# Column order and a 64-byte shift in the row-wise matrix products of a one-layer hybrid decoder

## Chip, cores and metric

The kernel runs on one core of one Trainium2 chip. The metric is the device time of one execution in microseconds (us), taken as the median of several runs.

## What is computed

One decoder layer on 256 tokens of width 2048, all in float32. The input projection has 5728 columns, the output projection maps 2048 to 2048, and the MLP goes from 2048 to 8192 and back. These four products are nearly all of the arithmetic:

```python
def hybrid_layer(x, g_mix, w_in, ..., w_out, g_mlp, w_up, w_down):
    h = rmsnorm(x, g_mix) @ w_in                 # 2048 x 5728
    ...
    x = x + jnp.concatenate([y_ssd, y_att], axis=-1) @ w_out   # 2048 x 2048
    u = rmsnorm(x, g_mlp) @ w_up                 # 2048 x 8192
    return x + jnp.square(jax.nn.relu(u)) @ w_down   # 8192 x 2048
```

Between the input and the output projection lie a state-space scan with a short convolution, and an attention over the 64 keys that a small indexer picks. The change touches neither.

## The kernel before

**Three matmuls for one.** A float32 product is computed with matmuls on the type `float32r`. Each operand is split into a high part that this type holds exactly and a low part that is the remainder, and each product becomes three: high by high, low by high, high by low. The weights come from memory as float32 in tiles named `raw`; `operands` (L113) loads them with a DMA on SP's queue (L122), ScalarE (ACT) writes the high part (L125) and VectorE (DVE) the low part (L126), both into one tile `w2`. There are 4 buffers of `raw` and 5 of `w2`, so the weights of several steps are ready ahead of TensorE.

**Two kinds of product.** In `product` (L138) the tokens end up on partitions: the stationary operand is 128 columns of activations (`hx`, `yah`, `ysh` or `uh`, with their low parts), the moving operand is the weights, 512 columns of a row of `w2` (304 in the two blocks `m0` and `m1` of the input projection), and the result is one accumulator of 512 columns in PSUM for each half of the tokens. For each of 16 slices `kt` of the inner dimension it issues six matmuls, L148 to L150 for the first 128 tokens and again for the others; one `operands` call serves two slices, that is 12 matmuls. In `product_t` (L184) it is the other way round: 128 columns of weights are stationary, and 256 tokens move (L200).

**Blocks.** The input projection is the blocks `k`, `m0`, `qi` (four calls of `product_t`), `xbc` (six calls), `m1`, `q0`, `q1`, `z0` and `z1`. Then come four blocks of `w_out`, 32 calls of `product_t` for `w_up` and 16 blocks of `product` for `w_down`. So 25 blocks of `product` are 512 columns wide, at 96 matmuls each, and two are 304 columns wide, also at 96. The last block of `w_down` is special: it has a `tail`, is cut into halves of 256 columns, and keeps four slices back so that its rows can leave early.

**Places.** Every large tile that TensorE reads (`hx`, `x2x`, `uh`, `ul`, `yah`, `yal`, `ysh`, `ysl`, `kih`, `kil`, `qis`, and each buffer of `w2`) starts at byte 224 of a 256-byte stretch of its partition; two unused tiles (L217, L219) see to that for the long-lived ones. A `shift` moves the weights inside `w2`: by 16 columns (64 bytes) for `product_t` (L188), by 48 columns for the block with the tail (L158), and by none for all other blocks of `product`. Below, the *place* of a matmul is the start of its moving operand minus the start of the next matmul's stationary operand, within 256 bytes. It is 0 in the 512-wide blocks of `product`, minus 64 in `product_t` and in the halves of the tail block, 0 for the indexer's matmuls (L465, and L466 for the most part), and in the 304-wide blocks, whose rows are not a whole number of 256 bytes, it goes through 0, minus 64, plus 64 and 128.

The order of TensorE's work is written out by hand: `step()` lets side tasks (transposes, the scan, the attention) put their matmuls between those of the products.

Of the kernel before, what the change touches and what calls it, by code (L numbers as in the profile page):

```python
# [9 lines left out]
F32 = mybir.dt.float32  # L10
F32R = mybir.dt.float32r
I32 = mybir.dt.int32
AF = mybir.ActivationFunctionType
OP = mybir.AluOpType
AX = mybir.AxisListType

P = 128
# [12 lines left out]
WB = 5  # L30
RB = 4

SPARE = 64
SHIFT_T = 16


Z0, XBC0, DT0, Q0, K0, V0, QI0, KI0, WI0, END = (
# [31 lines left out]
def hymba_kernel(ctx: ExitStack, tc: tile.TileContext, xn, xt, w_in, w_out, w_up, w_down, vcol, vrow, out):  # L69
    nc = tc.nc  # L70
    ctx.enter_context(tc.manual_schedule(engines={nc.tensor.engine}))
    keep = ctx.enter_context(tc.tile_pool(name="keep", bufs=1))
    wts = ctx.enter_context(tc.tile_pool(name="wts", bufs=1))
# [24 lines left out]
    def step():  # L98
        for t in list(tasks):
            if isinstance(t[1], int) and t[1] > 0:  # L100
                t[1] -= 1
            elif not isinstance(t[1], str) or t[1] in done:
                advance(t)
# [6 lines left out]
        return vc[:, VC[name] + i:VC[name] + i + 1]  # L110


    def operands(src, n, load=None, shift=0):  # L113

        with tc.high_priority(offset=HP):
            raw = wts.tile([P, n], F32, name="raw", tag="raw", bufs=RB)
            both = wts.tile([P, 2 * n + SPARE], F32R, name="w2", tag="w2", bufs=WB)
            hi, lo = both[:, shift:shift + n], both[:, shift + n:shift + 2 * n]
            step = n if load is None else n // 2
            for i in range(0, n, step):  # L120
                s = slice(i, i + step)
                nc.sync.dma_start(raw[:, s], src[:, s])  # L122
                if load is not None:
                    load()
                nc.scalar.copy(hi[:, s], raw[:, s])  # L125
                nc.vector.tensor_tensor(lo[:, s], raw[:, s], hi[:, s].bitcast(F32), op=OP.subtract)  # L126
        return hi, lo

    other = []
# [1 line left out]
    def mp(name):  # L131
        other.append(name)
        return ps.tile([P, 512], F32, name=name, tag="mid")

    def accumulator():
        return ps.tile([P, 512], F32, name="acc", tag="acc")

    def product(src, n, left, load=None, tail=None):  # L138


        acc = [accumulator(), accumulator()]
        last = KT if tail is None else KT - 4

        def part(kt, out, b, wh, wl):
            s = slice(b * P, (b + 1) * P)
            ah, al = left(kt)
            free = tail is not None
            nc.tensor.matmul(out, ah[:, s], wh, start=(kt == 0), stop=False, skip_group_check=free)  # L148
            nc.tensor.matmul(out, al[:, s], wh, start=False, stop=False, skip_group_check=free)  # L149
            nc.tensor.matmul(out, ah[:, s], wl, start=False, stop=(kt == KT - 1), skip_group_check=free)  # L150

        kept = []
        halves = [slice(0, n // 2), slice(n // 2, n)]
        if tail is not None:
            acc.append(mp("acc_t"))
        for kt in range(KT):
            if kt % 2 == 0:
                hi, lo = operands(src[kt // 2], 2 * n, load, 0 if tail is None else SPARE - SHIFT_T)  # L158
            w = slice(kt % 2 * n, kt % 2 * n + n)
            wh, wl = hi[:, w], lo[:, w]  # L160
            if tail is None:
                for b in range(NB):
                    part(kt, acc[b][:, :n], b, wh, wl)
            elif kt < last:
                for c in halves if kt else [slice(0, n)]:
                    part(kt, acc[0][:, c], 0, wh[:, c], wl[:, c])
                for i, c in enumerate(halves):
                    part(kt, acc[1 + i][:, c], 1, wh[:, c], wl[:, c])
            else:
                kept.append((kt, wh, wl))  # L170
            step()
        if tail is not None:
            for kt, wh, wl in kept:
                for c in halves:
                    part(kt, acc[0][:, c], 0, wh[:, c], wl[:, c])
            tail(0, slice(0, n), acc[0])
            for i, c in enumerate(halves):
                for kt, wh, wl in kept:
                    part(kt, acc[1 + i][:, c], 1, wh[:, c], wl[:, c])
                tail(1, c, acc[1 + i][:, c])  # L180
        other.append("product")
        return acc

    def product_t(src, right):  # L184

        acc = accumulator().rearrange("p (c t) -> p c t", c=2)
        for i in range(4):
            hi, lo = operands(src[i], 1024, shift=SHIFT_T)  # L188
            c = i % 2
            for k in range(8):  # L190
                kt = 8 * (i // 2) + k
                x = right(kt)
                s = slice(k * P, (k + 1) * P)
                todo = [(hi, 0, 0, T), (lo, 0, 0, T), (hi, 0, T, T)]

                if other:
                    other.clear()
                    todo[:1] = [(hi, 0, 0, P), (hi, P, P, T - P)]
                for j, (w, at, fr, n) in enumerate(todo):
                    nc.tensor.matmul(acc[:, c, at:at + n], w[:, s], x[:, fr:fr + n], start=(i + k + j == 0),  # L200
                                     stop=(i >= 2 and k == 7 and j == len(todo) - 1), skip_group_check=True)
                if k % 4 == 3:
                    step()
        return acc
# [47 lines left out]
    for name, cols in IN_BLOCKS:  # L252
        n = sum(b - a for a, b in cols)
# [3 lines left out]
    def in_block(name, load=None):  # L257
        o, n = in_off[name]
        src = w_in[o:o + n * D].rearrange("(g p c) -> g p c", g=8, p=P)
        return product(src, n, h_left, load)  # L260

    def in_pair(name, i):
        o = in_off[name][0] + i * 256 * D
        return product_t(w_in[o:o + 256 * D].rearrange("(h p c) -> h p c", h=4, p=P), lambda kt: hx[:, kt, :])
# [430 lines left out]
    def run():  # L695
# [58 lines left out]
        for j in range(4):  # L754
            spawn(residual(j, product(w_out[j], 512, y_left)), f"res{j}")
# [4 lines left out]
    def x2(kt):  # L760
        if kt >= KT - 4:
            need("res3")
        return box[0][:, kt, :]

    first = product_t(w_up[0], x2)
    while tasks:
        step()
# [11 lines left out]
    def up(q):  # L779
        uh = mlp.tile([P, KT, T], F32R, name="uh")  # L780
        ul = mlp.tile([P, KT, T], F32R, name="ul")
        for j in range(8):
            r = mlp.tile([P, 2, T], F32, name="r")
            acc = first if q + j == 0 else product_t(w_up[8 * q + j], x2)
            nc.scalar.activation(r, acc, AF.Relu)
            nc.vector.tensor_tensor(r, r, acc, op=OP.mult)
            s = slice(2 * j, 2 * j + 2)
            nc.scalar.copy(uh[:, s, :], r)
            nc.vector.tensor_tensor(ul[:, s, :], r, uh[:, s, :].bitcast(F32), op=OP.subtract)
        return uh, ul  # L790

    def down(q, u):
        for j in range(4):

            def add(b, c, acc):
                c = slice(512 * j + c.start, 512 * j + c.stop)
                nc.vector.scalar_tensor_tensor(xr[:, b, c], acc, rs4[:, b:b + 1], xr[:, b, c], op0=OP.mult, op1=OP.add)  # L797
                if q == 3:
                    nc.sync.dma_start(out[b * P:(b + 1) * P, c], xr[:, b, c])

            end = q == 3 and j == 3
            acc = product(w_down[4 * q + j], 512, lambda kt: (u[0][:, kt, :], u[1][:, kt, :]), tail=add if end else None)
            for b in range(0 if end else NB):
                add(b, slice(0, 512), acc[b])
# [58 lines left out]
```

## Time and profile before

| What | us |
|---|---|
| Median of 3 runs | 1092.11 (1091.97 to 1092.82) |
| The profiled execution, its own time | 1092.74 |
| Its span, first to last instruction | 1090.7 |
| TensorE busy in the span | 1084.6 (99%) |
| DVE busy | 657.5 (60%) |
| ACT busy | 526.6 (48%) |

TensorE is busy all the time by this table, but the duration of a matmul row holds its way through the array, which overlaps with the next matmul. What one matmul costs a full engine is the distance from its start to the next start, and that is what is read below from the timeline. The trace has lost a few records (7098 matmul rows of the program's 7214), so distances are taken from stretches without a gap.

### The profile page before, as it was taken

What the parts mean: (1) busy time and instruction counts of PE and PEld (TensorE: products, weight loads), DVE (VectorE), ACT (ScalarE), POOL (GpSimd) and SP (SyncE); (2) the same over time, 40 slices, a digit from 0 to 9 for tenths busy, and PEclk for the clock granted to TensorE, in tenths of its full rate; (3) what the DMA queues carried; (4) which work ended last, traced back from release to release, by engine and by line L of the source; (5) the groups of instructions that cost most, each with busy time, mean ns of one, the idle gap of its engine ahead of it and who ended that gap; (6) DMA issues with size and microseconds to landing.
All of it is one profiled execution on the core that took longest, in us unless ns stands there. A gap on an engine that the chain in (4) does not pass through costs nothing.

```text
span 1090.7 us, 17557 instructions
## 1 busy us (share of the span) xinstructions
PE 1084.6 (99%) x7098; PEld 987.5 (91%) x7098; DVE 657.5 (60%) x907; ACT 526.6 (48%) x693; POOL 24.3 (2%) x30
## 2 busy tenths in 40 slices
PE   9999999999999999999999999999999999999998
PEld 7999999888888899999998889998889999888888
DVE  6776898677765565555554455555445555454443
ACT  7745455456755454444443334444334444333331
POOL 0020000122000000000000000000000000000000
PEclk9999999999999999999999999999999999999999
DMA  9865447543475566666666666666666666666662
GB/s 311 272 207 179 153 127 223 165 145 126 135 251 191 176 187 196 195 193 194 195 193 194 193 193 193 193 194 193 194 193 193 193 194 193 194 193 193 213 213 76
DMA packets 63744, 207.52 MB, mean 190 GB/s; under 512 B 7216, under 2 KB 11568, under 8 KB 63664
## 3 DMA queue, kind: packets, MB, share of 16 engines
q1 hardware_dynamic: 63520, 206.36, 59.8%
q8 instruction: 55, 0.90, 0.4%
q14 instruction: 25, 0.20, 0.1%
q10 hardware_dynamic: 144, 0.05, 0.0%
HBM read 204.29 MB, written 2.10 MB: 189 GB/s over the span
## 4 chain that ended last, share of the span: by engine, by line
PE 95%; DVE 2%; DMA 1%; ACT 1%; issue 1%; SPq 0%; ACTq 0%; DVEq 0%
PE acc L200 41%; PE acc L148 16%; PE acc L150 16%; PE acc L149 16%; DVE w L126 1%; PE ps_y L575 1%; DMA xrow<-in_xn 1%; PE ps_sr L659 0%; PE ps_l L613 0%; PE ps_o L638 0%; DMA raw<-in_w_in 0%; ACT xrow L245 0%; DMA xT<-in_xt 0%; PE ps_s L465 0%; PE ps_s L466 0%
## 5 line engine op out<-in xcount | busy, mean ns | idle before, releaser
L126 DVE TENSOR_TENSOR w<-raw,w 128x1024 fp32r<-128x1024 f32 (+3 forms) x400 | 466.4, 1168 | 403.2 <-ACT w L125 402.7
L125 ACT CAST w<-raw 128x1024 fp32r<-128x1024 f32 (+3 forms) x400 | 399.8, 1003 | 504.0 <-PE acc L150 256.3
L200 PE MATMUL acc<-x2x,w 128*128 128x256 f32 (+1 forms) x3077 | 349.8, 276 | 0.0
L200 PEld LDWEIGHTS acc<-x2x,w 128*128 128x128 f32 x3077 | 349.4, 188 | 0.2
L148 PE MATMUL acc<-w,uh 128*128 128x512 f32 (+1 forms) x527 | 199.9, 379 | 0.0
L149 PE MATMUL acc<-w,ul 128*128 128x512 f32 (+1 forms) x527 | 199.8, 379 | 0.0
L150 PE MATMUL acc<-w,uh 128*128 128x512 f32 (+1 forms) x527 | 199.8, 379 | 0.0
L150 PEld LDWEIGHTS acc<-w,uh 128*128 128x128 f32 x527 | 98.9, 188 | 18.8
L149 PEld LDWEIGHTS acc<-w,ul 128*128 128x128 f32 x527 | 98.9, 188 | 18.7
L148 PEld LDWEIGHTS acc<-w,uh 128*128 128x128 f32 x527 | 98.9, 188 | 18.6
L200 PE MATMUL acc<-hx,w 128*128 128x256 f32 (+1 forms) x978 | 115.0, 277 | 0.0
L200 PEld LDWEIGHTS acc<-hx,w 128*128 128x128 f32 x978 | 112.8, 188 | 0.0
L148 PE MATMUL acc<-w,hx 128*128 128x512 f32 (+1 forms) x224 | 85.0, 379 | 0.4 <-ACT w L125 0.4
L150 PE MATMUL acc<-w,hx 128*128 128x512 f32 (+1 forms) x224 | 82.0, 366 | 0.0
L149 PE MATMUL acc<-w,hx 128*128 128x512 f32 (+1 forms) x224 | 81.9, 366 | 0.0
L148 PEld LDWEIGHTS acc<-w,hx 128*128 128x128 f32 x224 | 42.2, 189 | 7.2 <-ACT w L125 0.8
L150 PEld LDWEIGHTS acc<-w,hx 128*128 128x128 f32 x224 | 42.2, 188 | 7.0 <-DVE w L126 0.4
L149 PEld LDWEIGHTS acc<-w,hx 128*128 128x128 f32 x224 | 42.2, 188 | 6.6 <-issue 0.7
L797 DVE SCALAR_TENSOR_TENSOR xr<-acc,rs,xr 128x512 f32<-128x512 f32 (+1 forms) x32 | 22.3, 736 | 9.2 <-PE acc L150 9.2
L148 PE MATMUL acc<-w,yah 128*128 128x512 f32 x64 | 25.7, 402 | 0.0
L148 PE MATMUL acc<-w,ysh 128*128 128x512 f32 x64 | 25.1, 392 | 0.0
L150 PE MATMUL acc<-w,yah 128*128 128x512 f32 x64 | 25.0, 391 | 0.0
(214 smaller groups left out, 663.1 us busy)
## 6 DMA issues: line engine op xcount, KB each, us to landing
raw<-in_w_up SPq DMA_DIRECT2D x128, 512.0 KB, 4.3
raw<-in_w_down SPq DMA_DIRECT2D x128, 512.0 KB, 4.3
raw<-in_w_in SPq DMA_DIRECT2D x72, 512.0 KB, 3.6
raw<-in_w_out SPq DMA_DIRECT2D x32, 512.0 KB, 3.4
raw<-in_w_in SPq DMA_DIRECT2D x16, 256.0 KB, 4.3
raw<-in_w_in SPq DMA_DIRECT2D x16, 152.0 KB, 5.3
raw<-in_w_in SPq DMA_DIRECT2D x8, 304.0 KB, 2.9
xT<-in_xt SPq DMA_DIRECT2D x16, 128.0 KB, 4.2
```

The source lines that it names most:

```text
L125: nc.scalar.copy(hi[:, s], raw[:, s])
L126: nc.vector.tensor_tensor(lo[:, s], raw[:, s], hi[:, s].bitcast(F32), op=OP.subtract)
L148: nc.tensor.matmul(out, ah[:, s], wh, start=(kt == 0), stop=False, skip_group_check=free)
L149: nc.tensor.matmul(out, al[:, s], wh, start=False, stop=False, skip_group_check=free)
L150: nc.tensor.matmul(out, ah[:, s], wl, start=False, stop=(kt == KT - 1), skip_group_check=free)
L200: nc.tensor.matmul(acc[:, c, at:at + n], w[:, s], x[:, fr:fr + n], start=(i + k + j == 0), stop=(i >= 2 and k == 7 and j == len(todo) - 1) ...
L575: nc.tensor.matmul(pt[:, 64 * i:64 * i + 64], m[i // 4][:, i % 4, :], xdt[:, c, 64 * h:64 * h + 64], start=True, stop=True)
L797: nc.vector.scalar_tensor_tensor(xr[:, b, c], acc, rs4[:, b:b + 1], xr[:, b, c], op0=OP.mult, op1=OP.add)
```

## The change

In `product`, except in the block with the tail, the moving operand and the accumulator are no longer walked through from the first column to the last. `walk` turns both into the same pattern of three nested steps: 4 neighbouring columns (16 bytes), then 16 columns (64 bytes) further the next 4, and so on to the end of the row, and then again from column 4, from column 8 and from column 12. Every column is read once and its result lands where it did before; only the order within one matmul is another. The weights of these blocks start 16 columns further in `w2`, so that their place becomes plus 64. The rows of `raw` and `w2` in the 304-wide blocks are laid out at a distance of 320 columns, so that all of their rows have that place too; DMA, ACT and DVE then handle two runs of 304 columns where one of 608 stood (in `m1`; `m0` already came in halves). `product_t` and the block with the tail keep places and order.

No instruction is added, removed or moved on any engine; those concerned have other access patterns.

```diff
-SHIFT_T = 16
+SHIFT = 16
+
+RUN = 4
+STRIDE = 16
...
-    def operands(src, n, load=None, shift=0):
-
+    def operands(src, n, load=None, shift=0, parts=2):
+
+        pitch = (n + 63) // 64 * 64
         with tc.high_priority(offset=HP):
-            raw = wts.tile([P, n], F32, name="raw", tag="raw", bufs=RB)
-            both = wts.tile([P, 2 * n + SPARE], F32R, name="w2", tag="w2", bufs=WB)
-            hi, lo = both[:, shift:shift + n], both[:, shift + n:shift + 2 * n]
-            step = n if load is None else n // 2
-            for i in range(0, n, step):
+            raw = wts.tile([P, parts, pitch], F32, name="raw", tag="raw", bufs=RB)
+            both = wts.tile([P, 2 * parts * pitch + SPARE], F32R, name="w2", tag="w2", bufs=WB)
+            hi, lo = (both[:, shift + i * parts * pitch:shift + (i + 1) * parts * pitch]
+                      .rearrange("p (k c) -> p k c", k=parts)[:, :, :n] for i in range(2))
+            src = src.rearrange("p (k c) -> p k c", k=parts)
+            step = parts if load is None else 1
+            for i in range(0, parts, step):
                 s = slice(i, i + step)
-                nc.sync.dma_start(raw[:, s], src[:, s])
+                nc.sync.dma_start(raw[:, s, :n], src[:, s])
...
+    def walk(a):
+
+        return a.rearrange("p (c k i) -> p k c i", k=STRIDE // RUN, i=RUN)
...
             free = tail is not None
+            if not free:
+                out, wh, wl = walk(out), walk(wh), walk(wl)
             nc.tensor.matmul(out, ah[:, s], wh, start=(kt == 0), stop=False, skip_group_check=free)
...
-                hi, lo = operands(src[kt // 2], 2 * n, load, 0 if tail is None else SPARE - SHIFT_T)
-            w = slice(kt % 2 * n, kt % 2 * n + n)
-            wh, wl = hi[:, w], lo[:, w]
+                hi, lo = operands(src[kt // 2], n, load, SHIFT if tail is None else SPARE - SHIFT)
+            wh, wl = hi[:, kt % 2], lo[:, kt % 2]
...
-            hi, lo = operands(src[i], 1024, shift=SHIFT_T)
+            hi, lo = operands(src[i], 1024, shift=SHIFT, parts=1)
```

## Rows read from the trace of the kernel before

**Rows 1.** The page: busy time, and the chain that ended last.

```profile
span 1090.7 us, 17557 instructions
PE 1084.6 (99%) x7098; PEld 987.5 (91%) x7098; DVE 657.5 (60%) x907; ACT 526.6 (48%) x693; POOL 24.3 (2%) x30
...
PE 95%; DVE 2%; DMA 1%; ACT 1%; issue 1%; SPq 0%; ACTq 0%; DVEq 0%
PE acc L200 41%; PE acc L148 16%; PE acc L150 16%; PE acc L149 16%; DVE w L126 1%; PE ps_y L575 1%; DMA xrow<-in_xn 1%; PE ps_sr L659 0%; PE ps_l L613 0%; PE ps_o L638 0%; DMA raw<-in_w_in 0%; ACT xrow L245 0%; DMA xT<-in_xt 0%; PE ps_s L465 0%; PE ps_s L466 0%
```

**Rows 2.** Timeline of TensorE, 599.6 to 604 us (20 matmuls): start, duration, engine, line, operation.

```profile
599.63 0.39 PE L150 MATMUL acc<-w,uh 128*128 128x512 f32 x1
599.86 0.39 PE L148 MATMUL acc<-w,uh 128*128 128x512 f32 x1
599.86 0.19 PEld L149 LDWEIGHTS acc<-w,ul 128*128 128x128 f32 x1
...
603.94 0.39 PE L148 MATMUL acc<-w,uh 128*128 128x512 f32 x1
```

**Rows 3.** Timeline of TensorE, 559.8 to 564.5 us (41 alike merged in one row).

```profile
559.82 4.81 PE L200 MATMUL acc<-x2x,w 128*128 128x256 f32 x41
564.47 0.40 PE L148 MATMUL acc<-w,uh 128*128 128x512 f32 x1
```

**Rows 4.** Timeline of TensorE, 99.1 to 100.2 us (8 starts from first to last row).

```profile
99.15 0.28 PE L465 MATMUL ps_s<-kih,qis 128*128 128x256 f32 x1
...
100.11 1.09 PE L200 MATMUL acc<-hx,w 128*128 128x128 f32 x8
```

**Rows 5.** Timeline of TensorE, 256.2 to 258.2 us (each instruction recorded twice).

```profile
256.41 1.89 PE L638 MATMUL ps_o<-pT,room 128*128 128x256 f32 x8
258.13 0.27 PE L630 MATMUL ps_pt<-ident,L 128*128 128x128 f32 x1
```

**Rows 6.** Groups by shape, TensorE, whole span: count | busy us, mean ns | idle before.

```profile
L149 PE MATMUL acc<-w,ul 128*128 128x512 f32 x481 | 187.2, 389 | 0.0
...
L150 PE MATMUL acc<-w,hx 128*128 128x304 f32 x64 | 19.4, 302 | 0.0
...
L149 PE MATMUL acc<-w,hx 128*128 128x304 f32 x64 | 19.2, 300 | 0.0
...
L465 PE MATMUL ps_s<-kih,qis 128*128 128x256 f32 x32 | 8.0, 283 | 0.0
...
L566 PE MATMUL ps_dec<-vv,gtr 128*128 128x512 f32 x16 | 5.0, 392 | 0.0
...
L148 PE MATMUL acc_t<-w,uh 128*128 128x256 f32 x16 | 4.4, 276 | 0.0
```

**Rows 7.** Busy us (instructions) of PE, PEld, DVE, ACT, POOL; granted clock, DMA share, GB/s.

```profile
5.00:28.40 23.40, 23.01 (x99) 18.33 (x98) 18.27 (x41) 18.64 (x42) 0.00 (x0) 1.00 1.00 344
...
166.00:181.00 15.00, 15.00 (x111) 14.91 (x110) 14.76 (x34) 8.10 (x12) 0.00 (x0) 1.00 0.66 193
...
588.00:600.00 12.00, 12.00 (x55) 9.94 (x54) 5.67 (x5) 4.22 (x4) 0.00 (x0) 1.00 0.64 202
```

**Rows 8.** Waits, whole span: us in total, times, longest us.

```profile
ACT w L125 <- PE acc L150: 256.3, 158, 3.5
```

**Rows 9.** Groups by shape, ACT, whole span.

```profile
L125 ACT CAST w<-raw 128x1024 fp32r<-128x1024 f32 x360 | 378.3, 1052 | 493.5 <-PE acc L150 256.3 <-PE acc L200 140.0 <-issue 77.0
...
L125 ACT CAST w<-raw 128x304 fp32r<-128x304 f32 x16 | 6.3, 438 | 1.1 <-DMA raw<-in_w_in 1.1
```

**Rows 10.** Groups by shape, ACT, 166 to 181 us.

```profile
L125 ACT CAST w<-raw 128x608 fp32r<-128x608 f32 x4 | 2.7, 694 | 2.0 <-PE acc L200 2.0
```

**Rows 11.** Groups by shape, DVE, 166 to 181 us.

```profile
L126 DVE TENSOR_TENSOR w<-raw,w 128x608 fp32r<-128x608 f32 x5 | 3.9, 781 | 0.0
```

**Rows 12.** DMA issues of the page, one row: count, KB each, us to landing.

```profile
raw<-in_w_in SPq DMA_DIRECT2D x8, 304.0 KB, 2.9
```

More of the change, by code (lines that the diff above doesn't have):

```diff
@@ L110, in vcp @@
         return vc[:, VC[name] + i:VC[name] + i + 1]
-    def operands(src, n, load=None, shift=0):
+    def operands(src, n, load=None, shift=0, parts=2):
+        pitch = (n + 63) // 64 * 64
         with tc.high_priority(offset=HP):
-            raw = wts.tile([P, n], F32, name="raw", tag="raw", bufs=RB)
-            both = wts.tile([P, 2 * n + SPARE], F32R, name="w2", tag="w2", bufs=WB)
-            hi, lo = both[:, shift:shift + n], both[:, shift + n:shift + 2 * n]
-            step = n if load is None else n // 2
-            for i in range(0, n, step):
+            raw = wts.tile([P, parts, pitch], F32, name="raw", tag="raw", bufs=RB)
[5 more added lines that the diff above has]
+            for i in range(0, parts, step):
                 s = slice(i, i + step)
-                nc.sync.dma_start(raw[:, s], src[:, s])
+                nc.sync.dma_start(raw[:, s, :n], src[:, s])
                 if load is not None:
                     load()
-                nc.scalar.copy(hi[:, s], raw[:, s])
-                nc.vector.tensor_tensor(lo[:, s], raw[:, s], hi[:, s].bitcast(F32), op=OP.subtract)
+                nc.scalar.copy(hi[:, s], raw[:, s, :n])
+                nc.vector.tensor_tensor(lo[:, s], raw[:, s, :n], hi[:, s].bitcast(F32), op=OP.subtract)
         return hi, lo
@@ L199, in product_t @@
                 for j, (w, at, fr, n) in enumerate(todo):
-                    nc.tensor.matmul(acc[:, c, at:at + n], w[:, s], x[:, fr:fr + n], start=(i + k + j == 0),
+                    nc.tensor.matmul(acc[:, c, at:at + n], w[:, 0, s], x[:, fr:fr + n], start=(i + k + j == 0),
                                      stop=(i >= 2 and k == 7 and j == len(todo) - 1), skip_group_check=True)
```

## The prediction

> **What bounds the kernel.** I read the page first: TensorE is busy 99% of the span, and 95% of the chain that ended last is TensorE's, 41% on L200 and three times 16% on L148 to L150 [rows 1]. The waits come next: ACT, which makes the weights' high parts, spends 256 us waiting for L150 to give a weight buffer back [rows 8], so weights are ready before TensorE wants them. The windows show a granted clock of 1.00, that is 2.4 GHz, and DMA half to two thirds used, except in the first block, where it is full at 344 GB/s [rows 7]. So the time is the number of matmuls times the distance between their starts.
>
> That distance is the thing to look at. At 2.4 GHz 512 columns, one per cycle, take 213.3 ns. In a `w_down` block the starts go from 599.63 to 603.94 us in 19 steps: 226.8 ns [rows 2], 13.5 ns more than the columns take. In `product_t`, 256 columns would take 106.7 ns; 41 of them take 4.65 us, 113.4 each [rows 3], 6.7 ns over. The indexer has the same shape and type, 256 columns of `float32r`, and takes 0.96 us for 8, 120 each [rows 4], 13.3 ns over. I call this excess the toll. The groups show it too, since a row's mean duration is its distance plus some 162 ns (389 for 226.8, 276 for 113.4, 283 for 120) [rows 2 to 4, 6].
>
> Two readings fit. **By place:** the toll belongs to the weight load that runs beside each matmul (the load of L149 starts with the matmul of L148, at 599.86 [rows 2]), and the place of the two reads sets it: 13.5 and 13.3 ns at place 0, whether 512 or 256 columns long, and 6.7 at minus 64. The halves of the tail block, with weights moving as in `product`, but at minus 64, show 276 like `product_t` [rows 6]. **By column:** one cycle (0.417 ns) for every 64 bytes read gives 32 cycles or 13.3 ns for 512 columns and 6.7 for 256, and the indexer is an exception. I hold with the first: the indexer differs from `product_t` in place alone, and the 304-wide rows, at 301 on the mean of L149 and L150, that is 139 ns apart, have a toll of 12.3 over their 126.7 where the second would give 7.9 [rows 6].
>
> **The change, part by part.** Nothing is added or moved on any engine; 2304 matmuls of 512 columns and 192 of 304 get another order and place. Of the 2304, the 96 of block `k` run while DMA is full [rows 7]; what they save would be spent waiting for data, so I count 2208.
>
> *Order and place, on the path.* No row shows a walk in runs of 4 columns, nor the place plus 64 in a 512-wide matmul. From below, the toll can go to what a stream without such reads shows: L638, in plain float32, 8 records in 1.72 us, 215.0 each [rows 5], which at two cycles for each of its 256 columns is 213.3 and 1.7 over. That would save 226.8 - 215.0 = 11.8 ns. From above, a new place can cost: L566, 512 columns at another place (plus 160 for half of its loads), has 392 against 389, 3 ns more [rows 6]. The nearest row for taking two reads 64 bytes apart is the indexer against `product_t`, 120 - 113.4 = 6.6 ns for one weight load. I take that: 2208 x 6.6 ns = 14.6 us.
>
> *The 304-wide blocks.* 139 ns now, all at one place after; the same 6.6 ns give 192 x 6.6 = 1.3 us. Ends: minus 10.6 ns (down to 126.7 + 1.7), or plus 1, to the 302 of L150, whose places are plus 64 and 128; these are minus 2.0 and plus 0.2 us.
>
> *Making the weights.* In `m1` ACT and DVE take two runs of 304 instead of one of 608: between 694 ns and twice the 438 of a 304 form, 876 [rows 9, 10]; DVE similarly from 781 [rows 11]. At most some 0.2 us, eight times, on engines that are ahead: ACT waits for TensorE right there [rows 10]. The DMA of 304 KB [rows 12] gets two runs per partition; it lands in 2.9 us, and up to three more are under way. I cost these at nothing; without that cover it would be eight times 0.2, or 1.6 us. The 64 bytes' shift itself is only another address.
>
> *What is late next.* A step of 12 matmuls shrinks from 2.72 to 2.64 us. ACT needs 1.05 us of it [rows 9], DVE little more, and 512 KB in 2.64 us are 199 GB/s, under the 344 that the first block reaches [rows 7]. Nothing new becomes the bound; the end, in the tail block, is untouched.
>
> Sum: 14.6 + 1.3 = 15.9 us off the profiled execution's 1092.74, that is 1076.8; this execution was 0.6 above the median, so **1076.2 us**.
>
> **The rivals.**
>
> *Only a part or nothing is removed.* If the toll is by column after all, or if each group of 4 still meets the weight load as often as before, the time stays 1092.1. For it speaks the exact ratio of 13.5 to 6.7; against it the indexer. The Trainium skill (SBUF — State Buffer, Who interferes with whom) gives TensorE two independent read ports and says that it never waits on anyone; by that rule the place could do nothing, and the result would be this rival's. The 283 against 276 of one shape speak against that rule here [rows 6].
>
> *The place is the wrong one.* `product_t` and the tail have minus 64; the change makes plus 64. If that side meets the weight load more often and the walk doesn't help, each matmul pays like L566, 3 ns more: 2208 x 3 + 0.2 = 6.8 us, 1099 us. It decides as soon as the distance is above 226.8. For it speaks that L150's 304-wide rows, at plus 64 and 128, are 2 ns above L149's, at 0 and minus 64 [rows 6].
>
> *Each jump costs.* If the toll by column is the price of every entry into another 64-byte stretch, on the read or on the write side, the walk enters 128 times in a matmul and no longer 32: 96 x 0.417 = 40 ns for 512 columns, 57 x 0.417 = 23.8 for 304. That is 2208 x 40 + 192 x 23.8 = 92.9 us, and the time 1185. For it speaks the exact fit to one cycle per 64 bytes in both products. Against it: runs of 4 keep every 16 bytes together, and the indexer doesn't fit. The Trainium skill (PSUM — Partial Sum Buffer, Specifications (TRN2)) says that any non-contiguous access pattern slows matmuls significantly, since PSUM's lines are 8 bytes. By that rule this rival would happen; no matmul of this kernel writes PSUM with gaps, so no row here bears on it.
>
> **Chances and range.** Forecast 0.62, nothing 0.10, wrong place 0.13, jumps 0.15. A measurement of this kernel can tell some 0.2% (2.2 us) from no change: faster 0.62, within it 0.10, slower 0.28. The low end is the full toll gone, 11.8 x 2208 = 26.1 and 2.0 us, at 1064; the high end takes in the wrong place, 1100. The jumps are left out, with little else.
>
> **What would show it.** Right: L148 to L150 at 512 columns drop from 389 to about 382 ns, L200 stays at 276, the 304-wide rows come down to some 295, the three lines' share of the chain shrinks, and no engine but TensorE gains a wait. Only the place at work would show as a gain near 6.6 ns, the walk's own merit as more, up to 11.8. A mean of 392 would speak for the wrong place, one near 430 for the jumps, 389 for the toll by column. If the matmuls are shorter and the span is not, a supply of weights was closer to the bound than I read.

## The result, and the profile after the change

The changed kernel takes 1084.34 us (1083.87 to 1085.01) against 1092.46 us on the same chip, a ratio of 0.9925 with a 95% interval of 0.9908 to 0.9943: 8.1 us faster. The forecast was 1076.2 us, in a range from 1064 to 1100.

The page has the same shape as before: TensorE is busy all the time and makes up 95% of the chain that ended last [rows 1]. (All lines of `product` are 12 further down, those of `product_t` 11.)

```profile
span 1081.9 us, 17557 instructions
PE 1076.4 (99%) x7098; PEld 988.2 (91%) x7098; DVE 657.5 (61%) x907; ACT 525.6 (49%) x693; POOL 24.4 (2%) x30
...
PE 95%; DMA 2%; DVE 1%; ACT 1%; issue 1%; SPq 0%; ACTq 0%; DVEq 0%
PE acc L211 42%; PE acc L160 16%; PE acc L162 16%; PE acc L161 16%; DMA raw<-in_w_in 1%; DVE w L132 1%; PE ps_y L586 1%; DMA xrow<-in_xn 1%; PE ps_sr L670 0%; PE ps_l L624 0%; PE ps_o L649 0%; DMA xT<-in_xt 0%; PE ps_s L476 0%; PE ps_s L477 0%; PE ps_dec L577 0%
```

The distance from start to start has shrunk. The timeline of TensorE shows the first matmul of the second and of the third `w_down` block; between them lie the 96 matmuls of one block and nothing else. (Neither trace lacks a matmul of `product`: 96 are there for each block.) Columns are start, duration, engine, line, operation, tiles, shape.

```profile
582.05 0.38 PE L160 MATMUL acc<-w,uh 128*128 128x512 f32 x1
...
603.42 0.38 PE L160 MATMUL acc<-w,uh 128*128 128x512 f32 x1
```

That is 21.37 us for 96, or 222.6 ns, against 226.8 [rows 2]. The same two rows of the kernel before

```profile
586.26 0.39 PE L148 MATMUL acc<-w,uh 128*128 128x512 f32 x1
...
608.02 0.39 PE L148 MATMUL acc<-w,uh 128*128 128x512 f32 x1
```

are 21.76 us apart, 226.7 ns; this is how the distance in `w_down` is read for every run below. (The mean over all 15 blocks, which the expectations quote, is 222.7.) The groups by shape (count | busy us, mean ns | idle before) answer to [rows 6]:

```profile
L161 PE MATMUL acc<-w,ul 128*128 128x512 f32 x481 | 184.3, 383 | 0.0
...
L161 PE MATMUL acc<-w,hx 128*128 128x512 f32 x160 | 61.9, 387 | 0.0
...
L161 PE MATMUL acc<-w,yal 128*128 128x512 f32 x64 | 24.6, 384 | 0.0
...
L162 PE MATMUL acc<-w,hx 128*128 128x304 f32 x64 | 19.3, 302 | 0.1
L161 PE MATMUL acc<-w,hx 128*128 128x304 f32 x64 | 19.2, 300 | 0.0
...
L476 PE MATMUL ps_s<-kih,qis 128*128 128x256 f32 x32 | 8.0, 283 | 0.0
...
L577 PE MATMUL ps_dec<-vv,gtr 128*128 128x512 f32 x16 | 5.0, 392 | 0.0
...
L160 PE MATMUL acc_t<-w,uh 128*128 128x256 f32 x16 | 4.5, 281 | 0.0
```

The 512-wide rows went from 389 to 383 ns, those on `hx` (387) and `yal` (384) from 392 and 389. These 6 ns overstate the gain: a row of `w_down` lasted 162 ns longer than its distance before and lasts 160 longer after, and the distance fell by 4.1. The 304-wide ones, which were to fall to 295, stay at 300 and 302. What the change doesn't touch stays (L476 at 283, L577 at 392), with one exception: the halves of the tail block, same code at the same place, are at 281 where 276 stood. In the timeline of that block, 19 steps from the first to the second row:

```profile
1059.75 0.28 PE L162 MATMUL acc_t<-w,uh 128*128 128x256 f32 x1
...
1061.99 0.28 PE L160 MATMUL acc<-w,uh 128*128 128x256 f32 x1
```

2.24 us are 117.9 ns each (117.8 on the mean of the block), against 113.4 before.

**Where the time came from,** in means of the distance by group, without the steps that lead to another task's matmul: 1440 matmuls of `w_down` at 226.7 - 222.6 give 5.9 us; 384 of `q0` to `z1`, 228.4 to 224.0, give 1.7; 384 of `w_out`, 227.4 to 223.5, give 1.5. The tail block gives back 186 x 4.4 ns = 0.8 us, and `m1` 0.1 us (139.2 to 140.0). Block `k` and `m0` together end 0.2 us earlier: the first matmul of `product_t` starts at 41.82 us in the timeline of the kernel before,

```profile
41.82 0.50 PE L200 MATMUL acc<-hx,w 128*128 128x128 f32 x3
```

and at 41.58 us in that of the changed one.

```profile
41.58 0.64 PE L211 MATMUL acc<-hx,w 128*128 128x128 f32 x4
```

The sum is 8.4 us; the span shrank by 8.8, from 1090.7 to 1081.9.

**A step of 6.67 ns.** At 2.4 GHz 16 cycles take 6.67 ns. In that unit 226.7 ns are 34.0, 113.4 are 17.0 and 120 are 18; 222.6 are 33.4 or 167 for 5 matmuls, and 117.8 in the tail are 17 2/3 or 53 for 3. Single distances are not whole units. In the changed `w_down` they go round through 221, 224, 227, 224 and 217 ns, and such a round of five makes 167 units. The experiments below show other rounds: 236 and 231 ns (70 units) in plain order at minus 64; 226, 229 and 232 (103) in plain order at plus 64; 218, 230, 224 and 221 (134) in the walk at place 0. The kernel before is even, with 226 or 227 at every step. So what changes from setting to setting is the round that the matmuls fall into, and the sum of each of these rounds is a whole number of units.

### The profile page after: what moved, and what is told of

Same layout as the page of the kernel before. It is cut to its first block, busy times and chain, and to the rows that moved or that the text cites. A ratio compares the mean times of both kernels' runs of the same rounds, so it can differ in the third digit from the quotient of the medians.

```text
span 1081.9 us, 17557 instructions
## 1 busy us (share of the span) xinstructions
PE 1076.4 (99%) x7098; PEld 988.2 (91%) x7098; DVE 657.5 (61%) x907; ACT 525.6 (49%) x693; POOL 24.4 (2%) x30
## 4 chain that ended last, share of the span: by engine, by line
PE 95%; DMA 2%; DVE 1%; ACT 1%; issue 1%; SPq 0%; ACTq 0%; DVEq 0%
PE acc L211 42%; PE acc L160 16%; PE acc L162 16%; PE acc L161 16%; DMA raw<-in_w_in 1%; DVE w L132 1%; PE ps_y L586 1%; DMA xrow<-in_xn 1%; PE ps_sr L670 0%; PE ps_l L624 0%; PE ps_o L649 0%; DMA xT<-in_xt 0%; PE ps_s L476 0%; PE ps_s L477 0%; PE ps_dec L577 0%
## 5 line engine op out<-in xcount | busy, mean ns | idle before, releaser
L160 PE MATMUL acc<-w,uh 128*128 128x512 f32 (+1 forms) x527 | 197.2, 374 | 0.0
L161 PE MATMUL acc<-w,ul 128*128 128x512 f32 (+1 forms) x527 | 197.2, 374 | 0.0
L162 PE MATMUL acc<-w,uh 128*128 128x512 f32 (+1 forms) x527 | 197.2, 374 | 0.0
L160 PE MATMUL acc<-w,hx 128*128 128x512 f32 (+1 forms) x224 | 84.1, 376 | 0.4 <-ACT w L131 0.4
L161 PE MATMUL acc<-w,hx 128*128 128x512 f32 (+1 forms) x224 | 81.1, 362 | 0.0
L162 PE MATMUL acc<-w,hx 128*128 128x512 f32 (+1 forms) x224 | 80.9, 361 | 0.1
```

## The experiments

All runs but the kernel before are made from the changed kernel by the edits shown, some by two or three together (no walk and another place, say); the 304-wide blocks keep rows of 320 columns in all of them. Distance is that of the 512-wide matmuls in `w_down`, in ns and in units of 6.67 ns; the column "Tail" is that of the tail block's halves, whose code no run touches.

| Order of columns | Place | Distance, ns | Units | Tail, ns | Time, us | Ratio (95% interval) |
|---|---|---|---|---|---|---|
| Plain (kernel before) | 0 | 226.7 | 34.0 | 113.4 | 1092.5 | 1 |
| Plain | plus 64 | 228.9 | 34 1/3 | 113.4 | 1096.85 | 1.0037 (1.0024 to 1.0050) |
| Plain | minus 64 | 233.3 | 35.0 | 113.4 | 1106.09 | 1.0125 (1.0109 to 1.0140) |
| Walk | 0 | 223.3 | 33 1/2 | 113.4 | 1085.96 | 0.9939 (0.9923 to 0.9956) |
| Walk (changed kernel) | plus 64 | 222.6 | 33.4 | 117.8 | 1084.34 | 0.9925 (0.9908 to 0.9943) |
| Walk | minus 64 | 226.6 | 34.0 | 117.8 | 1101.15 | 1.0078 (1.0063 to 1.0093) |
| Walk | 128 | 230.0 | 34 1/2 | 117.8 | 1098.58 | 1.0050 (1.0033 to 1.0066) |
| Walk, reading only | plus 64 | 222.6 | 33.4 | 117.8 | 1084.42 | 0.9925 (0.9910 to 0.9940) |
| Walk, writing only | plus 64 | 228.9 | 34 1/3 | 113.4 | 1097.80 | 1.0043 (1.0026 to 1.0060) |
| Plain, half the weight load | 0 | 229.6 | 34.4 | 113.4 | 1098.12 | 1.0048 (1.0033 to 1.0063) |
| Plain, load at every second column | 0 | 233.3 | 35.0 | 113.4 | 1106.52 | 1.0126 (1.0111 to 1.0141) |
| Walk at 128 bytes | plus 64 | 240.0 | 36.0 | 113.4 | 1121.81 | 1.0267 (1.0252 to 1.0283) |
| Walk in runs of 8 | plus 64 | 235.5 | 35 1/3 | 113.4 | 1110.52 | 1.0155 (1.0139 to 1.0172) |
| Changed kernel, old block ahead of the tail | plus 64 | 222.6 | 33.4 | 113.4 | 1084.48 | 0.9925 (0.9911 to 0.9940) |

Each distance comes from one trace, but programs whose 512-wide reads are the same agree: three at 222.6 ns, two at 228.9. So differences of 2 ns and more in `w_down` belong to the settings and are not scatter.

### Place without the walk

```diff
-            if not free:
-                out, wh, wl = walk(out), walk(wh), walk(wl)
```

> The changed kernel without the walk: columns are read and written from the first to the last again, at place plus 64. Theory A (the place alone did it): the 512-wide matmuls of w_down stay near the 222.7 ns between starts that the changed kernel shows, and the time near 1084 us. Theory B (the walk alone did it): they return to 226.7 ns and the time to about 1092 us. Theory C (a step of 6.7 ns: a matmul of 512 columns takes 220.0 or 226.7 ns, and place and order choose how often which) only says that the mean lies from 220 to 227; it says so for all four runs of this set.

Measured: 1096.85 us. The two rows of the timeline, as above:

```profile
587.42 0.39 PE L158 MATMUL acc<-w,uh 128*128 128x512 f32 x1
...
609.40 0.39 PE L158 MATMUL acc<-w,uh 128*128 128x512 f32 x1
```

21.98 us for 96 are 228.9 ns, more than the 226.7 at place 0. The shift alone makes the kernel 0.4% slower; theory A falls for this place. Theory B is right that nothing is gained without the walk, but not in its 226.7, and theory C's upper end of 227 is passed. The same without the walk and with the shift at 48 columns:

```diff
-... SHIFT if tail is None else SPARE - SHIFT)
+... 48 if tail is None else SPARE - SHIFT)
```

> No walk, and the weights 48 columns further instead of 16, which is the place minus 64 of the transposed products and of the tail block. Theory A as the prediction had it: one 6.6 ns less per weight load, 220 ns between starts and about 1077 us. Theory B (walk alone): 226.7 ns, 1092 us. Theory C: 220 or 227 or a mix.

Measured: 1106.09 us, and in the timeline

```profile
590.46 0.40 PE L158 MATMUL acc<-w,uh 128*128 128x512 f32 x1
...
612.86 0.40 PE L158 MATMUL acc<-w,uh 128*128 128x512 f32 x1
```

22.40 us, 233.3 ns. This is the place that the prediction took for the good one, since `product_t` and the tail have it at 113.4 ns per 256 columns. In the 512-wide matmuls it is the worst of the three, by a whole unit. Theory A falls altogether, and none of the three gave this distance.

### The walk at other places

At place 0, with `0 if tail is None` in that line:

> The changed kernel with the weights of the row-wise products at place 0, as before the change, and with the walk. Theory A (place alone): 226.7 ns between starts in w_down and about 1092 us. Theory B (walk alone): near 222.7 ns and 1084 us. If both are needed, this run and the one without the walk both stay at 226.7. Theory C: a mean from 220 to 227 either way.

Measured: 1085.96 us.

```profile
583.47 0.38 PE L160 MATMUL acc<-w,uh 128*128 128x512 f32 x1
...
604.90 0.38 PE L160 MATMUL acc<-w,uh 128*128 128x512 f32 x1
```

21.43 us, 223.3 ns: theory B. Of the 4.1 ns that the change gained, the walk brings 3.4 by itself. In time, this run's interval and the changed kernel's overlap, so the shift's part on top of it is settled in the timeline alone.

At minus 64, with 48:

> The changed kernel with the weights 48 columns further instead of 16: the walk at place minus 64. Theory A (place): if minus 64 is the better side, 220 ns between starts and about 1077 us. Theory B (walk alone): as the changed kernel, 222.7 ns and 1084 us. Theory C: from 220 to 227 ns.

Measured: 1101.15 us.

```profile
587.81 0.38 PE L160 MATMUL acc<-w,uh 128*128 128x512 f32 x1
...
609.56 0.38 PE L160 MATMUL acc<-w,uh 128*128 128x512 f32 x1
```

21.75 us, 226.6 ns: at this place too the walk gains, 6.7 ns against plain order, but from 233.3. Theory B holds for the walk's sign, not for its result. The time is 8.4 us above the kernel before although `w_down` is as fast as there, and the groups by shape show why: the matmuls of `product_t`, the same code at the same place, have become longer.

```profile
L211 PE MATMUL acc<-x2x,w 128*128 128x256 f32 x3067 | 355.5, 279 | 0.0
```

The 279 ns instead of 276 are a mean of two kinds. Three stretches of `w_up` alternate with the blocks of `w_down`: the first, of 16 calls, stands ahead of them, the second and the third, of 8 calls each, follow directly behind a block. These are merged rows from the first and from the second stretch of this run (windows 520 to 530 and 690 to 700 us),

```profile
519.81 10.36 PE L211 MATMUL acc<-x2x,w 128*128 128x256 f32 x90
...
689.81 10.41 PE L211 MATMUL acc<-x2x,w 128*128 128x256 f32 x87
```

and this is the second stretch of the changed kernel, in the same window.

```profile
689.82 10.36 PE L211 MATMUL acc<-x2x,w 128*128 128x256 f32 x90
```

Without the 0.28 us that the last matmul of a row lasts, the steps are 113.3, 117.8 and 113.3 ns. In this run the two stretches behind `w_down`, some 1530 matmuls, run at 117.8, which makes 1530 x 4.4 ns = 6.7 us; the changed kernel's do not.

At place 128, with 32:

> The changed kernel with the weights 32 columns further instead of 16: the walk at place 128. So far the walk gave 223.4 ns in w_down at place 0, 222.7 at plus 64 and 226.7 at minus 64, each 3 to 7 ns under the plain order at the same place. If place works as a smooth offset, 128 lies between plus 64 and minus 64, at 223 to 227 ns and 1084 to 1100 us. If only the walk counts and minus 64 is the exception, it is 223 ns.

Measured: 1098.58 us.

```profile
587.45 0.39 PE L160 MATMUL acc<-w,uh 128*128 128x512 f32 x1
...
609.53 0.39 PE L160 MATMUL acc<-w,uh 128*128 128x512 f32 x1
```

22.08 us, 230.0 ns, worse than at all three other places. Place is no smooth offset, and minus 64 no exception; neither expectation held.

### Reading or writing

```diff
-                out, wh, wl = walk(out), walk(wh), walk(wl)
+                wh, wl = walk(wh), walk(wl)
+                out = walk(out) if n < 512 else out.rearrange("p (k c i) -> p k c i", k=4, i=RUN)
```

> The changed kernel, but in the 512-wide blocks only the weights are read in the order of the walk, while the accumulator is written from the first column to the last; the output's columns are thereby permuted within each block of 512, everything else is computed as before. Theory R (the toll is a meeting of two reads in SBUF): the distance in w_down stays at the changed kernel's 222.7 ns, since the write order is beside the point. Theory W (the toll sits at the writing of PSUM): back to the 228.9 ns that the run without the walk showed at the same place.

Measured: 1084.42 us.

```profile
584.21 0.38 PE L161 MATMUL acc<-w,uh 128*128 128x512 f32 x1
...
605.58 0.38 PE L161 MATMUL acc<-w,uh 128*128 128x512 f32 x1
```

21.37 us, 222.6 ns, the changed kernel's to the digit. The reverse walks `out` and gives `wh` and `wl` the plain order:

```diff
-                out, wh, wl = walk(out), walk(wh), walk(wl)
+                out = walk(out)
+                if n < 512:
+                    wh, wl = walk(wh), walk(wl)
+                else:
+                    wh, wl = (w.rearrange("p (k c i) -> p k c i", k=4, i=RUN) for w in (wh, wl))
```

> The reverse: in the 512-wide blocks the weights are read from the first column to the last, and only the accumulator is written in the order of the walk; the columns are permuted within each block of 512. Theory R (reads in SBUF): 228.9 ns as without the walk at this place, and some 1097 us. Theory W (writes to PSUM): 222.7 ns and 1084 us. If writing with gaps costs something of its own, it shows here as more than 228.9.

Measured: 1097.80 us.

```profile
588.94 0.39 PE L164 MATMUL acc<-w,uh 128*128 128x512 f32 x1
...
610.91 0.39 PE L164 MATMUL acc<-w,uh 128*128 128x512 f32 x1
```

21.97 us, 228.9 ns, as in plain order at this place. Theory R on both counts: the order of the reads does all of it, and the order of the writes nothing. Writing PSUM in runs of 4 at a step of 16 is free here.

### The weight load

```diff
             if not free:
-                out, wh, wl = walk(out), walk(wh), walk(wl)
+                if 0 < kt < KT - 1 and n == 512:
+                    s = slice(b * P, b * P + 64)
+                    out = out[:64]
...
-... SHIFT if tail is None else SPARE - SHIFT)
+... 0 if tail is None else SPARE - SHIFT)
```

> No walk and place 0, as before the change, but in 14 of the 16 slices of the 512-wide blocks the stationary operand has 64 columns instead of 128, so that a weight load reads half as much; the products of those slices for the second half of each 128 tokens are left out. Theory R by weight load (the excess over 213.3 ns belongs to the load beside the matmul): 226.7 falls by about half of its 13.4 ns, to 220. Theory by column (one cycle for each 64 bytes of the moving operand): 226.7 as before.

Measured: 1098.12 us. First the timeline, then the group of the short loads.

```profile
588.17 0.39 PE L162 MATMUL acc<-w,uh 128*128 128x512 f32 x1
...
610.21 0.39 PE L162 MATMUL acc<-w,uh 128*128 128x512 f32 x1
```

```profile
L163 PEld LDWEIGHTS acc<-w,ul 128*64 128x64 f32 x420 | 56.5, 134 | 39.2
```

In the kernel before the same group reads:

```profile
L149 PEld LDWEIGHTS acc<-w,ul 128*128 128x128 f32 x527 | 98.9, 188 | 18.7
```

The loads did become shorter, 134 ns instead of 188, but the distances didn't: 22.04 us are 229.6 ns, 2.9 more than with whole loads. This is a mean of two kinds: the two slices with whole loads keep their 226.7, and the 14 with half loads take 230.0 (34 1/2 units). The toll is not paid per column of the load. The run also halves the rows of the result, so it doesn't show which of the two brings the 3.3 ns more. The missing fall is against the prediction's reading by weight load in its simple form. It is no success of the reading by column either, which wanted 226.7.

```diff
-            s = slice(b * P, (b + 1) * P)
+            s = slice(b, T, 2) if n == 512 and not tail else slice(b * P, (b + 1) * P)
...
-            if not free:
-                out, wh, wl = walk(out), walk(wh), walk(wl)
...
-... SHIFT if tail is None else SPARE - SHIFT)
+... 0 if tail is None else SPARE - SHIFT)
```

> Place 0 and no walk, as before the change, but in the 512-wide blocks the stationary operand is every second column of 256, even tokens and then odd tokens, so that a weight load of 128 columns passes through 1024 bytes instead of 512; the tokens come out in another order, which leaves the masks and sums over tokens behind them without meaning. Theory R (the toll is a meeting of the moving read with the weight load): the distance changes from 226.7 ns, most likely upwards, since the load has twice as many 64-byte stretches to meet. Theory M (the moving read pays its toll by itself, as the run with half a load suggested): 226.7 ns, 1092 us.

Measured: 1106.52 us, in the same two views:

```profile
591.87 0.39 PE L158 MATMUL acc<-w,uh 128*128 128x512 f32 x1
...
614.27 0.39 PE L158 MATMUL acc<-w,uh 128*128 128x512 f32 x1
```

```profile
L159 PEld LDWEIGHTS acc<-w,ul 128*128 128x128 f32 x527 | 101.5, 193 | 19.3
```

22.40 us, 233.3 ns: with the moving read exactly as in the kernel before, other addresses of the load cost one whole unit, and the load itself is 193 instead of 188 ns, still shorter than the matmul beside it. So the load has a part in the toll, through its addresses. Theory M falls, and R stands in this much only: that the two reads meet is the likeliest reading, but no trace shows the meeting itself.

### Step and run of the walk

With `STRIDE = 32` for the 512-wide blocks:

> The changed kernel with a walk at a step of 32 columns (128 bytes) instead of 16 in the 512-wide blocks, runs of 4 as before, place plus 64; the 304-wide blocks keep their walk. If it matters only that neighbouring runs lie in different 64-byte stretches, 222.7 ns and 1084 us as with 64 bytes. If the step's own length matters, another mean from 220 to 233 ns, the span that all orders and places so far have shown.

Measured: 1121.81 us.

```profile
597.49 0.40 PE L161 MATMUL acc<-w,uh 128*128 128x512 f32 x1
...
620.52 0.40 PE L161 MATMUL acc<-w,uh 128*128 128x512 f32 x1
```

23.03 us, 240.0 ns, outside the span that I had named. With runs of 8 columns:

> The changed kernel with runs of 8 columns (32 bytes) at the same step of 64 bytes in the 512-wide blocks, place plus 64; the 304-wide blocks keep their runs of 4. If the walk helps by spreading the reads over 64-byte stretches, half as many changes of stretch give a mean between the plain order's 228.9 ns and the walk's 222.7. If the distance only has to come out as few steps of 6.7 ns as possible, it may also fall under 222.7, down to 220.0, and the time to some 1079 us; that would be the better version.

Measured: 1110.52 us.

```profile
593.57 0.40 PE L161 MATMUL acc<-w,uh 128*128 128x512 f32 x1
...
616.18 0.40 PE L161 MATMUL acc<-w,uh 128*128 128x512 f32 x1
```

22.61 us, 235.5 ns. Both expectations missed: neither does any walk over 64-byte stretches help, nor is something between plain and walk in between. Of the walks tried, only runs of 16 bytes at a step of 64 bytes gained. Both runs walk the reads and the writes alike, so they don't tell which of the two costs here. No version faster than the changed kernel was found.

### The tail block

```diff
-    def product(src, n, left, load=None, tail=None):
+    def product(src, n, left, load=None, tail=None, old=False):
...
-            if not free:
+            if not free and not old:
...
-... SHIFT if tail is None else SPARE - SHIFT)
+... (0 if old else SHIFT) if tail is None else SPARE - SHIFT)
...
+                          old=q == 3 and j == 2)
```

> The changed kernel, with the last 512-wide block of w_down, the one ahead of the tail block, at place 0 and without the walk. The tail block is the same code and the same addresses in both kernels, but its 256-column matmuls went from 113.4 to 117.8 ns. Theory H (a matmul stream inherits from the stream ahead of it how its reads fall): with the old block ahead the tail is back at 113.4 ns, and the old block itself at 226.7; the time is then within 1 us of the changed kernel's 1084. Theory against it (the tail's price comes from something else that the change moved): the tail stays at 117.8.

Measured: 1084.48 us. The tail block's halves, 35 steps from the first row to the second:

```profile
1057.77 0.28 PE L160 MATMUL acc<-w,uh 128*128 128x256 f32 x1
...
1061.74 0.28 PE L162 MATMUL acc_t<-w,uh 128*128 128x256 f32 x1
```

3.97 us, 113.4 ns. Theory H holds in this: the block ahead decides whether the tail runs at 117.8 or 113.4 ns, and the tail keeps that as long as it runs, here 186 matmuls. The table agrees: 117.8 stands wherever the block ahead is read in the change's walk at plus 64, minus 64 or 128, and 113.4 everywhere else. That it is the fall of the reads which is handed on is an interpretation. Nor is it a general rule: behind the same walk at plus 64 `product_t` stays at 113.4. Of the 0.8 us saved in the tail the old block's own 96 x 4.1 ns take back half, and the time is the same. The first block shows that the code ahead need not differ. Its matmuls, and all that the program has before them, are identical in this run and in the changed kernel; 46 steps of the changed kernel's timeline,

```profile
9.90 0.38 PE L161 MATMUL acc<-w,hx 128*128 128x512 f32 x1
...
20.02 0.38 PE L162 MATMUL acc<-w,hx 128*128 128x512 f32 x1
```

are 220.0 ns each, 33 units, and 46 steps of the same block here

```profile
9.87 0.38 PE L160 MATMUL acc<-w,hx 128*128 128x512 f32 x1
...
20.15 0.39 PE L161 MATMUL acc<-w,hx 128*128 128x512 f32 x1
```

are 223.5. What differs between the two is how the block begins: the changed kernel's steps are 427 ns or more up to 7.1 us, here they are short from 6.0 us on and TensorE then waits 0.35 us for ACT's weights, until 7.43 us. Whether that sets the round is not tested.

## Why the prediction was right, and where not

**What bounds the kernel** was read rightly: the distance between starts times their number gives 8.4 of the 8.8 us that the span lost. **What is late next** held too. ACT still waits for TensorE to free a buffer, 247 us instead of 256 [rows 8]:

```profile
ACT w L131 <- PE acc L162: 246.9, 158, 2.5
...
ACT w L131 <- DMA raw<-in_w_in: 6.4, 8, 1.4
```

The edits costed at nothing were worth nothing: ACT's casts in `m1` stay at 694 ns with two runs [rows 10],

```profile
L131 ACT CAST w<-raw 128x608 fp32r<-128x608 f32 x8 | 5.5, 694 | 7.6 <-PE acc L211 5.9 <-issue 1.8
```

and the DMA lands in 3.3 instead of 2.9 us [rows 12] under the same cover.

```profile
raw<-in_w_in SPq DMA_DIRECT2D x8, 304.0 KB, 3.3
```

Block `k` gained 1.0 us by itself (`m0` starts at 27.50 instead of 28.47 us) and gave most of it back in `m0`, where the weights were not there yet; leaving it out of the sum was right.

**The step that failed is the main term's reason,** "the place of the two reads sets it", and with it the 6.6 ns. It rests on the sentence that the indexer differs from `product_t` in place alone. That isn't so: the indexer's matmuls come 8 at a time, each two in a row load the same columns of `qis`, and a different stream stands ahead of them, a thing that moved the tail's 256 columns by 4.4 ns. So the difference, 120 and 113.4 ns [rows 3, 4], is real, but no run moved the indexer, and that its place makes it is not shown. To matmuls twice as long it doesn't carry over: there minus 64 costs 6.6 ns instead of saving as much, and plus 64 costs 2.2. The reading by column, which the prediction turned down, fell as well: it has one distance for 512 columns, and plain order showed three. The gain came from the other half of the change, which had no row: the walk, 3.4 ns at place 0 and 6.3 at plus 64, each against plain order at the same place. The term was 14.6 us and came to 9.1 (5.9, 1.7 and 1.5). The 6.6 ns were, unnoticed, one unit of 6.67 ns; the change saves 0.6 of a unit on the mean.

That the sign and the range held is therefore luck as far as the reason goes. What the 6.6 ns stood for, the new place, made the kernel 0.4% slower by itself, and the walk, which the sum did not price, made up for that and left a gain of 8.1 us, half of the forecast 15.9. The prediction's own mark of being right, a row mean of about 382 ns, was met by 383 without the distance having fallen by 6.6: the rows shrank by 6 ns and the distances by 4.1.

**The 304-wide blocks** were to give 1.3 us. `m0` went from 139.1 to 135.9 ns, most of which was spent waiting for weights, and `m1` lost 0.8 ns. There the walk costs: in the run with plain order at plus 64 `m1` takes 137.8 ns, and 140.0 with the walk. **The end "untouched"** was wrong: no instruction of the tail block changed, and it lost 0.8 us to the state that it inherited.

**The rivals.** *Wrong place* was half right: the place plus 64 does cost, 2.2 ns for the 3 that the rival put, but the walk more than makes up for it. *Each jump costs* fell: with 128 jumps at a step of 64 bytes the reads are faster, and the writes cost nothing. The Trainium skill's rule behind it (PSUM — Partial Sum Buffer, Specifications (TRN2)), that any non-contiguous pattern slows matmuls significantly, is not borne out for runs of 4 columns at a step of 16: 228.9 ns with and without gaps. *Nothing is removed* fell by the time. The Trainium skill's other rule, that TensorE never waits on anyone (SBUF — State Buffer, Who interferes with whom), sits badly with a weight load whose addresses alone take the distance from 226.7 to 233.3 ns; there the measurement decides.

**What stays open** is what exactly the moving read meets. Its own order matters, the load's addresses matter, a shorter load doesn't shorten it, and a round comes out as a whole number of units of 16 cycles. A rule that gives 33.4 for one setting and 36 for another was not found, and place within 256 bytes is not all of it: the changed kernel's one order and place gives 222.6 ns in `w_down`, 223.5 in `w_out` and 224.0 in `q0` to `z1`. Nor is it known what a stream hands on: behind the walk at minus 64 both `product_t` and the tail run slower, behind the walk at plus 64 only the tail.

## What to carry to other kernels

Where TensorE is full, compare the distance between starts with columns over clock: a toll of a few per cent in a tight stream of 4-byte operands depends on the order and the addresses of its reads, and can be tuned by access patterns alone, here by 0.7% of the time, without a single instruction more. Read it from the starts, since a row's duration can shrink by more than the distance does. Such a setting has to be measured at the very shape that will use it: the place at which 256 columns ran at 113.4 ns was the worst of three for 512. And look at the neighbours afterwards: untouched matmuls behind a changed stream may become slower or faster.

## What the runs showed of the hardware

Distances between `float32r` matmuls of 512 columns fall into rounds; in `w_down` they had one to six matmuls. The means of the rounds are simple fractions of 6.67 ns (16 cycles at 2.4 GHz): 33, 33.4, 33 1/2, 34, 34 1/3, 34 1/2, 35, 35 1/3 and 36 units were seen, and 17, 17 2/3 and 18 for 256 columns. Which one it is can persist: identical streams ran at 113.4 or 117.8 ns by what stood ahead of them, and identical first blocks at 220.0 or 223.5. Writing PSUM in runs of 16 bytes at a step of 64 cost nothing measurable (228.9 ns either way). Reading and writing in the same runs at a step of 128 took 240.0 ns, where plain order at the same place takes 228.9.
